# Rope tables and attention bias made in the third projection group, and a gate's blocks spread over three groups, in a one-core transformer layer

## The chip, the core and the metric

The kernel runs on one core of a Trainium2 chip. The core has a matrix engine (TensorE, PE in the profile, its weight loads PEld), a vector engine (VectorE, DVE), a scalar engine (ScalarE, ACT), a general engine (GpSimd, POOL) and a sync engine (SyncE, SP), which here only issues transfers. Each engine runs its own queue in order. The metric is device time in microseconds for one execution. The kernel before took 1390.01 us, the median of three runs (1387.78 to 1391.03).

## The reference

One layer of a diffusion transformer, 256 latent tokens and 256 context tokens of width 2048, all in float32. What matters here:

```python
mod = (silu_c @ w_ada[l] + b_ada[l])[:, None, :]           # 6 segments of 2048: shift, scale, gate, twice
sh_a, sc_a, gt_a, sh_f, sc_f, gt_f = jnp.split(mod, 6, axis=-1)
h  = rms_norm(x,  g_attn[l]) * (1.0 + sc_a)  + sh_a         # latent tokens
hc = rms_norm(xc, g_attn[l]) * (1.0 + csc_a) + csh_a        # context tokens
pl = jnp.split(h @ w_in, offsets, axis=-1)                  # w_in: 2048 x 4928, four head groups
pc = jnp.split(hc @ w_in, offsets, axis=-1)
# neighbourhood attention (bias rpb), grouped queries with rotary, latent attention, differential attention
x = x + gt_a * o_l                                          # gate of the attention: segment 2
h = rms_norm(x, g_ffn[l]) * (1.0 + sc_f) + sh_f             # segments 4 and 3
x = x + gt_f * swiglu(h, ffn_wg[l], ffn_wu[l], ffn_wd[l])   # segment 5
return rms_norm(x, g_final)
```

## The kernel before, in words

Every large product is done in split precision: a weight tile is loaded (512 KB, `raw`), ACT rounds it to a high part (`whi`, L137), DVE subtracts for the low part (`wlo`, L140), and PE makes three passes (L160, L161, L163). Weight tiles go through four `raw` buffers and six `whi`/`wlo` buffers, all loaded from SP's queue.

The input projection of the first head groups (queries, keys and values of the first, queries, keys and values of the second: five blocks of 512 columns, line 437 and `q_block`) is cut along the contraction into five groups, `parts = [[0], [1], [2, 3], [4, 5], [6, 7]]`, each number being a pair of 128-row chunks. Partial sums stay in SBUF and DVE adds each group's to them (L410). While a group runs, the shift and scale of the pairs of the next group are computed on PE (`ada_pe`, L296): a pair needs eight loads of w_ada (L198, "pair loads" below; each is two transfers of 256 KB), the first four into the four buffers `araw`, the next four into the four buffers `o` of another pool, which later hold the rope tables, the bias and the attention outputs. When a pair's shift and scale are there, `modulate` (L309 to L326) makes its normed activations, which the next group's products read.

The segments 2, 4 and 3 of the modulation (the first gate, then scale and shift of the second half) are needed for one token row only and are computed on DVE (`ada_block`): a segment is four blocks of 512 columns, and a block is eight loads of 512 KB ("gate loads" below), each followed by two multiply-adds over 128x512 on DVE (L374; the block's first product is on ACT, L372). `add_ada` puts the blocks in a queue of side tasks. `side.pump` is called after each step of the main work with an estimated cost; a block's next load and its multiply-adds are put into the program each time the estimated clock has moved on by `gap`:

```python
due[0] = max(due[0] + gap, side.now - 4 * gap)
yield 0.0, max(0.0, due[0] - side.now)
```

In the fifth group (`gi == len(parts) - 1`, L530) the kernel before calls `prepare()` (L458) and queues blocks 0 and 1 of the gate with a gap of 2.4, through the `araw` buffers. `prepare` loads the bias, the rope tables, the gains and the mask into `xa` and `xb` (buffers that the tokens have left), and POOL makes from them the tables `tab` and two tiles `bias`, in three of the four `o` buffers. Blocks 2 and 3 and the segments 4 and 3, ten blocks or 80 loads, follow the projection groups with a gap of 2.6 (L670 to L672), through the `raw` buffers that the weights also use. They run beside the attention heads and the remaining projections (`proj`: ML_CQ, DF_Q, ML_CKV, DF_K, DF_V). All of segment 2 must be done at L914, 4 and 3 at L953. The order of instructions on each engine is then settled by a list scheduler, which works with estimated durations.

Of the kernel before, what the change touches and what calls it, by code (L numbers as in the profile page):

```python
# [10 lines left out]
F32 = mybir.dt.float32  # L11
F32R = mybir.dt.float32r
AF = mybir.ActivationFunctionType
ALU = mybir.AluOpType
# [3 lines left out]
P = 128  # L18
# [69 lines left out]
def hybrid_dit_kernel(ctx: ExitStack, tc: tile.TileContext, a, out):  # L88
    nc = tc.nc
    pe, act, dve, pool, sp = nc.tensor, nc.scalar, nc.vector, nc.gpsimd, nc.sync  # L90
# [20 lines left out]
    opool = po.enter_context(tc.tile_pool(name="opool", bufs=1, side="right"))  # L111
# [276 lines left out]
    def add_ada(seg, gap, load, nbs=range(4), ahead=0):  # L388
        due[0] = side.now
        order = [(nb, k2) for nb in nbs for k2 in range(8)]  # L390
        held = {}

        def fetched(nb, k2):

            i = order.index((nb, k2))
            for nb_, k_ in order[i:i + ahead + 1]:
                if (nb_, k_) not in held:
                    c0 = seg * D + nb_ * 512
                    held[nb_, k_] = load(ada_rows[:, 2 * k_:2 * k_ + 2, c0:c0 + 512], [P, 2, 512])
            return held[nb, k2]  # L400

        return [side.add(ada_block(seg, nb, gap, load, fetched), lane="gate", width=1) for nb in nbs]
# [51 lines left out]
    tabs, bias = {}, []  # L454
# [3 lines left out]
    def prepare():  # L458

        xa = sb0.tile([P, 2, 4, S], F32, name="xa", tag="x_t", bufs=2)  # L460
        act.dma_start(xa, a["na_bias"].rearrange("t p h k -> p t h k"))
        xb = sb0.tile([P, D], F32, name="xb", tag="x_t", bufs=2)
        cs128 = xb[:, 0:512].rearrange("p (a t n) -> p a t n", a=2, t=2)
        act.dma_start(cs128[:, 0], a["rope_c128"].rearrange("(t p) n -> p t n", p=P))
        act.dma_start(cs128[:, 1], a["rope_s128"].rearrange("(t p) n -> p t n", p=P))
        gb = xb[:, 512:768].rearrange("p (t n) -> p t n", t=2)
        act.dma_start(gb[:, 0, :], a["gqa_gq"].partition_broadcast(P))
        act.dma_start(gb[:, 1, :], a["gqa_gk"].partition_broadcast(P))
        mask = xb[:, 768:832]
        act.dma_start(mask, a["na_mask"])  # L470
        lv = xb[0:64, 832:836]
        act.dma_start(lv, a["diff_l"].rearrange("t d -> d t"))
        lp = xb[0:64, 836:838]
        dve.tensor_tensor(out=lp, in0=lv[:, 0:2], in1=lv[:, 2:4], op=ALU.mult)
        lps = misc()
        pe.matmul(lps[:, 0:2], lhsT=ones[0:64, 0:1].to_broadcast([64, P]), rhs=lp, start=True, stop=True)
        act.activation(le, lps[:, 0:2], AF.Exp)
        dve.tensor_tensor(out=neglam, in0=le[:, 1:2], in1=le[:, 0:1], op=ALU.subtract)
        dve.tensor_scalar(out=neglam, in0=neglam, scalar1=-0.2, scalar2=None, op0=ALU.add)
        tab = opool.tile([P, 2, 2, 2, 128], F32, name="tab", tag="o", bufs=4)  # L480
        for i, nm in enumerate("qk"):
            cg, sg = tab[:, i, 0], tab[:, i, 1]
            g = gb[:, i:i + 1, :]
            pool.tensor_tensor(out=cg, in0=cs128[:, 0], in1=g.to_broadcast([P, 2, 128]), op=ALU.mult)
            for lo, hi in ((0, 64), (64, 0)):
                pool.tensor_tensor(out=sg[:, :, lo:lo + 64], in0=cs128[:, 1, :, lo:lo + 64], in1=g[:, :, hi:hi + 64].to_broadcast([P, 2, 64]), op=ALU.mult)
            tabs[nm] = (cg, sg)
        for t in range(2):
            b = opool.tile([P, 4, S], F32, name="bias", tag="o", bufs=4)
            bv = b.rearrange("p h (i c) -> p (h i) c", c=64)  # L490
            pool.tensor_tensor(out=bv, in0=xa[:, t].rearrange("p h (i c) -> p (h i) c", c=64), in1=mask.unsqueeze(1).to_broadcast([P, 16, 64]), op=ALU.add)
            bias.append(b)

    def first_group():
# [27 lines left out]
    gate_tasks = []  # L522
    for gi, prs in enumerate(parts):
        nxt = []
        if gi + 1 < len(parts):
            for pr in parts[gi + 1]:
                nxt.append(side.add(ada_pe(pr, wait=(3.0, 1.5, 5.5, 5.5)[gi]), lane="ada", width=1))
                if gi == 0:
                    nxt[-1]["ready"] = side.now + 8.0
        if gi == len(parts) - 1:  # L530
            prepare()
            gate_tasks = add_ada(2, 2.4, ada_raw, (0, 1))
        if gi == 0:
            first_group()
        else:
            q_block(prs, False)
            for c0, units in blocks:
                block(c0, prs, False, units)
        side.finish(*nxt)
        if gi + 1 < len(parts):  # L540
            for pr in parts[gi + 1]:
                modulate(pr)
# [124 lines left out]
        pool.dma_start(g, gd.partition_broadcast(P))  # L667
        return g

    GAP = 2.6  # L670
    gate_tasks = add_ada(2, GAP, stream_raw, (2, 3))
    mod_tasks = add_ada(4, GAP, stream_raw) + add_ada(3, GAP, stream_raw)  # L672

    act.activation(na_qT, na_qT, AF.Copy, scale=128.0 ** -0.5)
    sc_mm = plain_score(na_qT, na_kT, lambda h: h)
# [389 lines left out]
    for gi, (f0, f1) in enumerate(groups):  # L1065
        last = gi == len(groups) - 1
        aT, tasks = {}, {}
        for fb in range(f0, f1):
            ga = gu(a["ffn_wg"], fb) if fb else first_g
            sg = []  # L1070
# [43 lines left out]
    for t in range(2):  # L1114
        for c0, cn in (((0, 512),) if t == 0 else ((0, 256), (256, 256))):
# [5 lines left out]
            c = slice(3 * 512 + c0, 3 * 512 + c0 + cn)  # L1121
# [79 lines left out]
```

## Time and profile before

| | us |
|---|---|
| median of three runs | 1390.01 |
| the profiled execution, its own time | 1391.13 |
| span of its instructions | 1389.3 |
| PE busy | 1344.1 |
| DVE busy | 916.3 |
| ACT busy | 618.9 |
| POOL busy | 60.6 |

The profile is of one execution, and all rows below are of it. PE is busy for 97% of the span, so what can be won is in the few stretches in which it isn't. In the rows of stretches each engine has its busy time and, in brackets, its instructions; then the granted TensorE clock (1.00 is 2.4 GHz), the busy share of the transfer engines and what they moved in GB/s. Times are from the start of the span. The third group runs from 91.16 to 142.84 us, the fourth to 195.50, the fifth to about 247. At 219.67 SP issues the first weight load of ML_CQ and at 369.7 the last of ML_CKV.

### The profile page before, as it was taken

What the parts mean: (1) busy time and instruction counts of PE and PEld (TensorE: products, weight loads), DVE (VectorE), ACT (ScalarE), POOL (GpSimd) and SP (SyncE); (2) the same over time, 40 slices, a digit from 0 to 9 for tenths busy, and PEclk for the clock granted to TensorE, in tenths of its full rate; (3) what the DMA queues carried; (4) which work ended last, traced back from release to release, by engine and by line L of the source; (5) the groups of instructions that cost most, each with busy time, mean ns of one, the idle gap of its engine ahead of it and who ended that gap; (6) DMA issues with size and microseconds to landing.
All of it is one profiled execution on the core that took longest, in us unless ns stands there. A gap on an engine that the chain in (4) does not pass through costs nothing.

```text
span 1389.3 us, 19890 instructions
## 1 busy us (share of the span) xinstructions
PE 1344.1 (97%) x7082; PEld 1088.9 (78%) x7082; DVE 916.3 (66%) x1623; ACT 618.9 (45%) x1180; POOL 60.6 (4%) x78
## 2 busy tenths in 40 slices
PE   6999999988999999999999999999999999999997
PEld 4788878766877587787888888888888888888886
DVE  4474589987787936769697855445555565555575
ACT  4432233553233526548444444444444444444453
POOL 1000030100010000000221000000000000000000
PEclk9999999999999999999999999999999999999999
DMA  9998867577878746445899766666565656666554
GB/s 368 333 360 283 278 225 225 171 253 228 279 229 295 248 134 213 136 126 194 308 371 325 246 188 195 187 194 190 189 196 184 217 180 209 196 186 193 189 171 142
DMA packets 179511, 313.78 MB, mean 226 GB/s; under 512 B 14002, under 2 KB 53972, under 8 KB 178260
## 3 DMA queue, kind: packets, MB, share of 16 engines
q1 hardware_dynamic: 170400, 285.25, 62.7%
q0 software_dynamic: 5664, 24.14, 4.6%
q10 hardware_dynamic: 3348, 3.13, 0.8%
q8 instruction: 55, 0.90, 0.3%
q14 instruction: 44, 0.36, 0.1%
HBM read 310.36 MB, written 2.11 MB: 225 GB/s over the span
## 4 chain that ended last, share of the span: by engine, by line
PE 77%; DVE 10%; DMA 8%; issue 3%; ACT 2%; POOL 1%; ACTq 0%; SPq 0%; POOLq 0%; DVEq 0%
PE acc L160 24%; PE acc L161 23%; PE acc L163 23%; DVE ada_acc L374 3%; DMA raw<-in_w_ada_dram 3%; DVE wlo L140 2%; DMA raw<-in_w_in_dram 2%; PE m L296 2%; POOL rstd L172 1%; PE m L1050 1%; PE m L878 1%; DMA x_t<-in_ctx_dram 1%; PE m L589 1%; ACT whi L137 1%; PE m L640 1%
## 5 line engine op out<-in xcount | busy, mean ns | idle before, releaser
L140 DVE TENSOR_TENSOR wlo<-raw,whi 128x512 fp32r<-128x512 f32 (+1 forms) x764 | 492.5, 683 | 354.2 <-ACT whi L137 348.1
L137 ACT CAST whi<-raw 128x512 fp32r<-128x512 f32 (+1 forms) x764 | 433.7, 615 | 572.6 <-PE acc L161 437.2
L160 PE MATMUL acc<-whi,h_hi 128*128 128x512 f32 x704 | 275.1, 391 | 0.0
L161 PE MATMUL acc<-whi,h_lo 128*128 128x512 f32 x704 | 274.1, 389 | 0.0
L163 PE MATMUL acc<-wlo,h_hi 128*128 128x512 f32 x704 | 190.6, 390 | 0.0
L160 PE MATMUL acc<-whi,h 128*128 128x512 f32 (+1 forms) x416 | 165.4, 402 | 8.0 <-ACT whi L137 5.6
L161 PE MATMUL acc<-whi,h 128*128 128x512 f32 (+1 forms) x416 | 159.1, 385 | 0.0
L163 PEld LDWEIGHTS acc<-wlo,h_hi 128*128 128x128 f32 x704 | 132.2, 188 | 28.0 <-DVE wlo L140 0.5
L161 PEld LDWEIGHTS acc<-whi,h_lo 128*128 128x128 f32 x704 | 132.2, 188 | 27.1
L160 PEld LDWEIGHTS acc<-whi,h_hi 128*128 128x128 f32 x704 | 132.2, 188 | 27.0
L160 PE MATMUL acc<-whi,ah 128*128 128x512 f32 (+1 forms) x364 | 139.0, 383 | 0.0
L161 PE MATMUL acc<-whi,al 128*128 128x512 f32 (+1 forms) x364 | 138.6, 382 | 0.0
L374 DVE SCALAR_TENSOR_TENSOR ada_acc<-raw,cs,ada_acc 128x512 f32<-128x512 f32 x150 | 112.1, 749 | 15.0 <-DMA raw<-in_w_ada_dram 8.3
L163 PE MATMUL acc<-wlo,h 128*128 128x512 f32 (+1 forms) x416 | 117.4, 385 | 1.1 <-DVE wlo L140 1.0
L160 PEld LDWEIGHTS acc<-whi,h 128*128 128x128 f32 x416 | 79.5, 192 | 30.9 <-ACT whi L137 10.5
L163 PE MATMUL acc<-wlo,ah 128*128 128x512 f32 (+1 forms) x364 | 96.2, 382 | 0.0
L161 PEld LDWEIGHTS acc<-whi,h 128*128 128x128 f32 x416 | 80.0, 192 | 13.8 <-issue 1.4
L163 PEld LDWEIGHTS acc<-wlo,h 128*128 128x128 f32 x416 | 76.8, 190 | 17.1 <-DVE wlo L140 3.1
L160 PEld LDWEIGHTS acc<-whi,ah 128*128 128x128 f32 x364 | 68.4, 188 | 13.3
L161 PEld LDWEIGHTS acc<-whi,al 128*128 128x128 f32 x364 | 68.5, 188 | 13.1
L163 PEld LDWEIGHTS acc<-wlo,ah 128*128 128x128 f32 x364 | 67.6, 188 | 13.3
L160 PE MATMUL acc<-whi,o_hi 128*128 128x512 f32 x128 | 51.4, 403 | 0.0
(231 smaller groups left out, 1343.4 us busy)
## 6 DMA issues: line engine op xcount, KB each, us to landing
raw<-in_ffn_wg_dram SPq DMA_DIRECT2D x88, 512.0 KB, 4.4
raw<-in_ffn_wu_dram SPq DMA_DIRECT2D x88, 512.0 KB, 4.2
raw<-in_ffn_wd_dram SPq DMA_DIRECT2D x88, 512.0 KB, 4.2
raw<-in_w_ada_dram SPq DMA_DIRECT2D x80, 512.0 KB, 4.6
raw<-in_w_in_dram SPq DMA_DIRECT2D x72, 512.0 KB, 5.5
araw<-in_w_ada_dram SPq DMA_DIRECT2D x128, 256.0 KB, 5.4
raw<-in_w_out_dram SPq DMA_DIRECT2D x32, 512.0 KB, 3.7
graw<-in_w_ada_dram POOLq DMA_DIRECT2D x32, 512.0 KB, 6.3
```

The costliest lines, as they stand in the source:

```text
L137: act.copy(hi, raw[:, k])
L140: dve.tensor_tensor(out=lo, in0=raw[:, k], in1=hi.bitcast(F32), op=ALU.subtract)
L160: pe.matmul(dst, lhsT=l[0], rhs=r[0], start=start, stop=False)
L161: pe.matmul(dst, lhsT=l[0 if w_left else 1], rhs=r[1 if w_left else 0], start=False, stop=False)
L163: pe.matmul(dst, lhsT=l[1 if w_left else 0], rhs=r[0 if w_left else 1], start=False, stop=stop)
L172: pool.tensor_tensor(out=r[:, :n], in0=v[:, :n], in1=mhalf[:, :n], op=ALU.pow)
L296: pe.matmul(mv[32 * j:32 * j + 32, :P], lhsT=cs32[:, kc, :], rhs=raw[:, kc % 2, j // 2, tsl(j % 2)], start=(kc == 0), stop=(kc == KC - 1), ...
L374: dve.scalar_tensor_tensor(out=acc_, in0=raw[:, kk, :], scalar=cs[:, 0, kc:kc + 1], in1=acc_, op0=ALU.mult, op1=ALU.add)
L589: pe.transpose(ps[:, tsl(j)], src[:, tsl(j)], ident)
L640: pe.matmul(o[:, :S], lhsT=vt(kc)[:, v0:v0 + P], rhs=pT[:, kc, :], start=(kc == 0), stop=(kc == 3))
L878: pe.matmul(sc, lhsT=df_qT[hb, h, tsl(t)], rhs=df_kT[h // 2][hb, h % 2, :], start=True, stop=True)
L1050: pe.transpose(ps[:, tsl(j)], src[:, tsl(j)], ident)
```

## The change

`prepare` is called in the third group instead of the fifth. It now makes the tables and the bias where their inputs lie, in `xb` and `xa`, on POOL as before. A new function `keep`, called in the fifth group, copies them into the three `o` buffers on ACT. Blocks 0 and 1 of the gate are queued in the third group with a gap of 7.0, block 2 in the fifth with a gap of 3.0 (all through `araw`), and block 3 and the segments 4 and 3 after the groups with gaps of 3.6, 3.6 and 2.8 (were 2.6).

```diff
-        tab = opool.tile([P, 2, 2, 2, 128], F32, name="tab", tag="o", bufs=4)
+        tab = xb[:, 1024:2048].rearrange("p (i s t n) -> p i s t n", i=2, s=2, t=2)
...
+        for t in range(2):
+            bv = xa[:, t].rearrange("p h (i c) -> p (h i) c", c=64)
+            pool.tensor_tensor(out=bv, in0=bv, in1=mask.unsqueeze(1).to_broadcast([P, 16, 64]), op=ALU.add)
+        return xa, xb
+
+    def keep(xa, xb):
+
+        tab = opool.tile([P, 2, 2, 2, 128], F32, name="tab", tag="o", bufs=4)
+        act.copy(tab.rearrange("p i s t n -> p (i s t n)"), xb[:, 1024:2048])
+        for i, nm in enumerate("qk"):
+            tabs[nm] = (tab[:, i, 0], tab[:, i, 1])
         for t in range(2):
             b = opool.tile([P, 4, S], F32, name="bias", tag="o", bufs=4)
-            bv = b.rearrange("p h (i c) -> p (h i) c", c=64)
-            pool.tensor_tensor(out=bv, in0=xa[:, t].rearrange("p h (i c) -> p (h i) c", c=64), in1=mask.unsqueeze(1).to_broadcast([P, 16, 64]), op=ALU.add)
+            act.copy(b, xa[:, t])
             bias.append(b)
...
+        if gi == 2:
+            made = prepare()
+            gate_tasks = add_ada(2, 7.0, ada_raw, (0, 1))
         if gi == len(parts) - 1:
-            prepare()
-            gate_tasks = add_ada(2, 2.4, ada_raw, (0, 1))
+            keep(*made)
+            gate_tasks += add_ada(2, 3.0, ada_raw, (2,))
...
-    GAP = 2.6
-    gate_tasks = add_ada(2, GAP, stream_raw, (2, 3))
-    mod_tasks = add_ada(4, GAP, stream_raw) + add_ada(3, GAP, stream_raw)
+    gate_tasks = add_ada(2, 3.6, stream_raw, (3,))
+    mod_tasks = add_ada(4, 3.6, stream_raw) + add_ada(3, 2.8, stream_raw)
```

On SP's queue in the third and fourth group, first as it was and then as it is (L125 loads weights, L198 are pair loads, two rows of `x2` each half a pair, L276 are gate loads):

```order
L125 DMA raw<-in_w_in_dram 128x2x512 x4
L198 DMA araw<-in_w_ada_dram 128x2x256 x8
L125 DMA raw<-in_w_in_dram 128x2x512
L198 DMA araw<-in_w_ada_dram 128x2x256 x8
L125 DMA raw<-in_w_in_dram 128x2x512 x4
```

```order
L125 DMA raw<-in_w_in_dram 128x2x512 x4
L276 DMA araw<-in_w_ada_dram 128x2x512 x4
L198 DMA araw<-in_w_ada_dram 128x2x256 x4
L125 DMA raw<-in_w_in_dram 128x2x512
L198 DMA araw<-in_w_ada_dram 128x2x256 x4
L125 DMA raw<-in_w_in_dram 128x2x512
L198 DMA araw<-in_w_ada_dram 128x2x256 x8
L125 DMA raw<-in_w_in_dram 128x2x512 x4
```

Four gate loads come ahead of a pair's first half; there are four such rounds, two in the third group and two in the fourth, and the pair loads behind them wait for the `araw` buffers that the gate loads' multiply-adds on DVE release.

On DVE's queue at the end of the third group, first as it was and then as it is (`gq_k`, `gq_v` and `kT` are partial sums, L309 begins the modulation for the next group):

```order
L410 TENSOR_TENSOR gq_k<-acc,gq_k 128x256
L410 TENSOR_TENSOR gq_v<-acc,gq_v 128x256
L140 TENSOR_TENSOR wlo<-raw,whi 128x512 x3
L410 TENSOR_TENSOR kT<-acc,kT 128x512 x3
L140 TENSOR_TENSOR wlo<-raw,whi 128x512
L410 TENSOR_TENSOR kT<-acc,kT 128x512
L309 TENSOR_TENSOR scg<-m,colA_147 128x4
```

```order
L374 SCALAR_TENSOR_TENSOR ada_acc<-araw,cs,ada_acc 128x512
L410 TENSOR_TENSOR gq_k<-acc,gq_k 128x256
L374 SCALAR_TENSOR_TENSOR ada_acc<-araw,cs,ada_acc 128x512
L410 TENSOR_TENSOR gq_v<-acc,gq_v 128x256
L374 SCALAR_TENSOR_TENSOR ada_acc<-araw,cs,ada_acc 128x512
L140 TENSOR_TENSOR wlo<-raw,whi 128x512
L374 SCALAR_TENSOR_TENSOR ada_acc<-araw,cs,ada_acc 128x512 x2
L140 TENSOR_TENSOR wlo<-raw,whi 128x512
L374 SCALAR_TENSOR_TENSOR ada_acc<-araw,cs,ada_acc 128x512
L140 TENSOR_TENSOR wlo<-raw,whi 128x512
L374 SCALAR_TENSOR_TENSOR ada_acc<-araw,cs,ada_acc 128x512 x2
L410 TENSOR_TENSOR kT<-acc,kT 128x512 x3
```

Eight multiply-adds now stand between the last partial sums of one block and the first of the next.

On SP's queue in DF_Q, first as it was and then as it is (`w_in` rows are weight loads, `w_ada` rows are gate loads):

```order
L125 DMA raw<-in_w_in_dram 128x2x512
L125 DMA raw<-in_w_ada_dram 128x2x512 x2
L125 DMA raw<-in_w_in_dram 128x2x512
L125 DMA raw<-in_w_ada_dram 128x2x512 x2
L125 DMA raw<-in_w_in_dram 128x2x512
L125 DMA raw<-in_w_ada_dram 128x2x512 x3
L125 DMA raw<-in_w_in_dram 128x2x512
```

```order
L125 DMA raw<-in_w_in_dram 128x2x512
L125 DMA raw<-in_w_ada_dram 128x2x512
L125 DMA raw<-in_w_in_dram 128x2x512
L125 DMA raw<-in_w_ada_dram 128x2x512
L125 DMA raw<-in_w_in_dram 128x2x512
L125 DMA raw<-in_w_ada_dram 128x2x512 x2
L125 DMA raw<-in_w_in_dram 128x2x512
```

Fewer gate loads stand between two weight loads. From the first weight load of ML_CQ to the last of ML_CKV there were 44 of them and are 30; in DF_K there were 33 and are 28; in DF_V there were 5 and are 14.

## Rows read from the trace of the kernel before

**Rows 1.** The page: the chain that ended last, by engine.

```profile
PE 77%; DVE 10%; DMA 8%; issue 3%; ACT 2%; POOL 1%; ACTq 0%; SPq 0%; POOLq 0%; DVEq 0%
```

**Rows 2.** Busy time by stretch: stretch, length, engines, clock, transfers.

```profile
75.00:100.00 25.00, 24.86 (x242) 21.02 (x242) 21.93 (x48) 10.31 (x19) 0.00 (x0) 1.00 1.03 374
91.16:142.84 51.68, 51.54 (x467) 42.70 (x465) 27.76 (x53) 13.43 (x25) 0.00 (x0) 1.00 0.87 293
142.84:195.50 52.66, 52.66 (x476) 43.69 (x475) 35.52 (x65) 14.88 (x28) 6.49 (x7) 1.00 0.81 271
195.50:219.67 24.17, 21.14 (x104) 17.36 (x103) 23.46 (x39) 10.33 (x18) 4.85 (x2) 0.86 0.62 196
219.67:369.68 150.01, 137.44 (x645) 106.80 (x644) 133.01 (x269) 64.03 (x137) 9.37 (x8) 0.98 0.69 224
369.68:470.00 100.32, 94.80 (x463) 75.03 (x463) 81.52 (x155) 37.90 (x86) 3.60 (x4) 0.97 0.81 263
470.00:525.00 55.00, 55.00 (x244) 41.38 (x243) 27.00 (x47) 20.62 (x45) 0.00 (x0) 1.00 0.54 172
```

**Rows 3.** The chain between 219.67 and 369.68 us, by line.

```profile
by line: DVE ada_acc L374 17.8%; DMA raw<-in_w_ada_dram 15.0%; DMA raw<-in_w_in_dram 13.5%; DVE wlo L140 9.2%; issue 8.4%; POOL rstd L172 3.9%; PE acc L160 2.8%; PE m L731 2.5%; DVE st L616 2.5%; PE acc L161 2.4%; PE acc L163 2.1%; DVE m L6
```

**Rows 4.** What ACT waited for from 219.67 to 369.68: us, times, longest.

```profile
ACT whi L137 <- DMA raw<-in_w_in_dram: 28.1, 14, 3.8
```

**Rows 5.** What SP waited for from 219.67 to 369.68.

```profile
SPq L125 <- DVE wlo L140: 66.0, 26, 8.8
```

**Rows 6.** Transfers issued from 219.67 to 369.68: count, size, median us to landing.

```profile
raw<-in_w_ada_dram SPq DMA_DIRECT2D x40, 512.0 KB, 4.5
raw<-in_w_in_dram SPq DMA_DIRECT2D x16, 512.0 KB, 4.7
raw<-in_w_in_dram SPq DMA_DIRECT2D x7, 320.0 KB, 3.9
araw<-in_w_ada_dram SPq DMA_DIRECT2D x2, 512.0 KB, 5.6
```

**Rows 7.** PE's wait from 195.5 to 219.67.

```profile
PE acc L160 <- DVE kT L410: 3.0, 2, 1.6
```

**Rows 8.** DVE in order of time, 194 to 204.

```profile
195.87 2.26 DVE L374 SCALAR_TENSOR_TENSOR ada_acc<-araw,cs,ada_acc 128x512 f32<-128x512 f32 x1
198.06 0.68 DVE L410 TENSOR_TENSOR kT<-acc,kT 128x512 f32<-128x512 f32 x1
198.66 2.24 DVE L374 SCALAR_TENSOR_TENSOR ada_acc<-araw,cs,ada_acc 128x512 f32<-128x512 f32 x1
```

**Rows 9.** The multiply-adds of L374 alone, from 219.67 to 369.68.

```profile
219.67:369.68 150.01, 61.96 (x83) 0.98 0.69 224
```

**Rows 10.** POOL in order of time, 194 to 201: start, us, instruction.

```profile
194.76 5.59 POOL L491 TENSOR_TENSOR bias<-xa,xb 128x1024 f32<-128x1024 f32 x2
```

**Rows 11.** Transfers from 91.16 to 142.84: bytes and mean rate.

```profile
DMA packets 12668, 15.16 MB, mean 293 GB/s; under 512 B 746, under 2 KB 9847, under 8 KB 12663
```

**Rows 12.** The first gate loads on SP, 177 to 187.

```profile
180.05 6.78 SPq L276 DMA_DIRECT2D araw<-in_w_ada_dram  x5
```

**Rows 13.** ACT in order of time, 184 to 197.

```profile
184.93 0.72 ACT L372 ACTIVATE ada_acc<-araw,cs 128x512 f32<-128x512 f32 x1 [1.74 <-DMA araw<-in_w_ada_dram]
...
190.28 0.27 ACT L299 COPY mvs<-m 128x128 f32<-128x128 f32 x1 [1.64 <-PE m L296]
195.00 1.14 ACT L137 CAST whi<-raw 128x512 fp32r<-128x512 f32 x2 [4.46 <-PE acc L161]
```

**Rows 14.** ACT's issue of the mask, 58 to 63.6.

```profile
60.87 0.33 ACTq L470 DMA_DIRECT2D xb<-in_na_mask_dram  x1
```

**Rows 15.** DVE in order of time, 68 to 78.

```profile
74.12 1.38 DVE L140 TENSOR_TENSOR wlo<-raw,whi 128x512 fp32r<-128x512 f32 x2 [2.73 <-ACT whi L137]
```

**Rows 16.** An ACT pass over 128x1024.

```profile
212.28 1.06 ACT L674 ACTIVATE qT<-qT 128x1024 f32<-128x1024 f32 x1
```

**Rows 17.** PE's use of that `mvs` tile.

```profile
195.49 0.14 PEld L302 LDWEIGHTS m<-ident,mvs 128*128 128x128 f32 x1
```

More of the change, by code (lines that the diff above doesn't have):

```diff
@@ L486, in prepare @@
                 pool.tensor_tensor(out=sg[:, :, lo:lo + 64], in0=cs128[:, 1, :, lo:lo + 64], in1=g[:, :, hi:hi + 64].to_broadcast([P, 2, 64]), op=ALU.mult)
-            tabs[nm] = (cg, sg)
+        for t in range(2):
[7 more added lines that the diff above has]
+            tabs[nm] = (tab[:, i, 0], tab[:, i, 1])
         for t in range(2):
             b = opool.tile([P, 4, S], F32, name="bias", tag="o", bufs=4)
-            bv = b.rearrange("p h (i c) -> p (h i) c", c=64)
-            pool.tensor_tensor(out=bv, in0=xa[:, t].rearrange("p h (i c) -> p (h i) c", c=64), in1=mask.unsqueeze(1).to_broadcast([P, 16, 64]), op=ALU.add)
+            act.copy(b, xa[:, t])
             bias.append(b)
```

## The prediction

> **What bounds the kernel now.** I read the chain that ended last first. Three quarters of it are PE, then come DVE and the transfers [rows 1], and POOL has 1%. PE is busy for 1344.1 of 1389.3 us, so all that this change can win without touching a matmul is in 45.2 us, and the next view must say where they are. That is the table by stretch [rows 2]. The third and fourth group have almost none: PE idles 51.68 - 51.54 = 0.14 us and 0.00 us. The opening of the fifth has 24.17 - 21.14 = 3.03 us. The stretch of the attention heads and the first remaining projections, 219.67 to 369.68, has 150.01 - 137.44 = 12.57 us. The next hundred microseconds have 5.52, and 470 to 525 has none.
>
> In the long stretch I then read the chain by line: the multiply-adds of the gate loads 17.8%, the gate loads themselves 15.0%, the weight loads 13.5% [rows 3]. So loads in flight and their consumers end last there, not PE. The waits say the same from two sides: ACT waited 28.1 us for weights to land [rows 4], and SP waited 66.0 us for a raw buffer that DVE's subtraction had not released [rows 5]. The transfer engines are busy for 69% only; it is the ring of four buffers that is tight. In the transfers 40 + 2 gate loads stand beside 16 + 7 weight loads [rows 6], so 65 loads in 150.01 us, 2.31 us each.
>
> **The opening of the fifth group.** PE waited 3.0 us, twice, for an addition to kT [rows 7]. Two multiply-adds just ahead of these additions took 2.26 and 2.24 us [rows 8] in place of 61.96/83 = 0.75 us [rows 9], while POOL made its two bias passes, 5.59 us from 194.76 on [rows 10]. That is 1.51 + 1.49 = 3.0 us, the whole of PE's wait. POOL's passes leave this place, and ten multiply-adds of block 1 stand ahead of the modulation on DVE where twelve stood. I take -2.5 us; the bounds are 0 (these multiply-adds hold kT back just as long by their number) and -4 (3.03 and something of the following clock, which is 0.86 in this stretch).
>
> **The long stretch.** Its gate loads fall from 42 to some 30 (SP's order has 44 and 30 between the two weight loads that mark its ends; the trace's stretch holds 42 of the 44). If every load went on taking 2.31 us, 30 + 23 = 53 loads would take 122.3 us, 27.7 less; but PE's own work is 137.44 us, so the stretch can't shrink by more than 12.57 us unless PE's work gets shorter too, as it would if its clock (0.98) or its pipelining gained. DVE loses 12 x 2 x 0.7465 = 17.9 us, from 133.01 to 115.1, and 115.1/137.4 is 84%, which no longer binds. On the other side the chain also holds pieces that aren't side work: DVE's softmax steps, POOL's rstd, issue [rows 3]. If these filled the place of the loads, nothing would be won. I take most of PE's idle time and a little of the faster matmul stream, -12 us, between 0 and -27.7. The value is near the 12.57, since that is the row that PE itself gives.
>
> **Behind it.** In 369.68 to 470 there are five loads fewer (33, now 28) of 5.52 us of idle time; I take -0.5 us. From 470 to 525 nine more stand (5, now 14): 9 x 2 x 0.7465 = 13.4 us on DVE, which is busy for 27.0 of 55.0 us. PE's 55.0 busy us hide it: 0. If that cover were gone, the price would be those 13.4 us.
>
> **The third and fourth group.** Here the cost must lie. A gate load is 0.524 MB, so eight add 4.19 MB to the third group's 15.16 MB [rows 11]: 19.35 MB. The rate that this kernel held over 75 to 100 us is 374 GB/s [rows 2]; by it they need 51.7 us, exactly what the group takes. By 293 GB/s at a share of 0.87 the engines would be full at 337 GB/s and need 57.4 us, +5.7 us. The fourth group moved 0.271 x 52.66 = 14.3 MB, and with eight gate loads where some five stood, 1.6 MB more, it fits by either.
>
> The rate of 374 GB/s was held for 25 us [rows 2]. The Trainium skill's page "DMA: Bandwidth & Descriptors", section Specifications, puts the memory limit of one core at about 358 GB/s. By it 19.35 MB would need an estimated 54.05 us, 2.4 us more than the group takes; by the row it costs nothing. This trace goes above the page's figure, so the row stands.
>
> What the change adds is a wait. The pair loads on SP now stand behind four gate loads and want the same `araw` buffers, which DVE's multiply-adds release. Behind the waiting pair load are four weight loads, and PE needs those. On DVE the first multiply-add of a round waits for ACT's first product (L372) and that for the transfer; behind it stand evacuations (gq_k, gq_v, kT), wlo and the modulation. On ACT whi stands behind L372. Today five gate loads issued from 180.05 on [rows 12] gave ACT its input 4.88 us later, at 184.93, after an idle 1.74 us [rows 13]. A round is thus 4.9 us of landing and 8 x 0.7465 = 6.0 us on DVE, some 11 us; four rounds fit in 104 us, and DVE goes from 27.76 to some 39 busy us out of 51.68. I take +2 us in all for late weights or late partial sums, from 0 to +5.7.
>
> **POOL's passes, at another place.** The last of their inputs, the mask, was issued at 60.87 [rows 14]; with a gate load's 4.9 us it is there by 66, and `xa` and `xb` are free. So they should run between some 65 and 77 us, where DVE makes wlo (at 74.12, already 2.73 us after whi [rows 15]). One bias pass, 5.59/2 = 2.8 us, is the most that one wlo can be held by. I take +0.5 us, from 0 to +2.8.
>
> **The copies on ACT.** The copies are three of 128x1024, 1.06 us each by the nearest pass of that size [rows 16], 3.2 us. Two of them stand ahead of the copy of mvs, which ended at 190.28 + 0.27 [rows 13] and is used at 195.49 [rows 17]. With 2.1 us ahead it ends at 192.7, still in time, and ACT idled 4.46 us before its next rounding at 195.00 [rows 13]. So 0, at most +1.
>
> **The sum.** -2.5 - 12 - 0.5 + 0 + 2 + 0.5 + 0 = -12.5 us. The profiled execution's own time is 1391.13 us, 1.1 above the median of 1390.01. Its sum gives 1378.6, brought to the median 1377.5. I predict 1378 us.
>
> **The rivals.** *The relief is lost.* The long stretch is held by its own chains: statistics, softmax steps and the ring of buffers, in which one slow wlo holds the next load (8.8 us at worst [rows 5]). For it speaks that the rows of loads make up only 46% of the chain; against it, that DVE's share is 89% now. Then only the opening's 2.5 us are won and the groups' 2.5 us spent: 1390 to 1391 us.
>
> *More than the idle time.* If the time per load stays near 2.31 us and the waits of PE shrink in the matmul stream as well, the stretch gives 20 us, halfway to its bound and beyond PE's idle row: -2.5 - 20 - 0.5 + 2.5 = -20.5, 1370 us, 1369 from the median. For it speaks that SP waited 66.0 us for buffers; against it that the clock is already 0.98.
>
> *The rounds stall PE.* One mechanism: SP waits in order on a pair load until DVE has released `araw`, DVE waits until the gate loads have landed, and the four weight loads behind come late. It decides at PE's loss per round: four rounds that cost more than (15 + 2.8)/4 = 4.4 us each eat the gains of 2.5 + 12 + 0.5 and 0.2% of the time more. At 5 us each it is 1391.1 - 15 + 20 = 1396 us. For it speaks the third group's share of 0.87 in the transfer engines; against it that a round needs 11 of 26 us, and that PE idled 0.14 us in a group whose SP was already in order behind the same buffers.
>
> **Chances.** The forecast has 0.60, the lost relief 0.13 (of it 0.10 within 0.2%, which is about what a measurement of this kernel can tell from no change, and 0.03 faster), more than the idle time 0.17, the stalling rounds 0.10. So faster 0.80, same 0.10, slower 0.10. The range is 1366 to 1391 us, the forecast's own 1372 to 1386. The low end is -4 in the opening and -20 in the stretch; the high end takes in the lost relief, and also a stretch that gives 4 us with +5.7 in the groups (1390.0 - 2.5 - 4 - 0.5 + 5.7 = 1388.7). Left out are the stalls, 0.10, and some 0.07 of still larger gains.
>
> **What would show it.** In the new profile PE's idle time from the fifth group's first product to ML_CQ's first weight load should be below 1 us with no multiply-add above 1 us there; the long stretch should have about 53 loads and PE's idle time at 1 to 3 us, with DVE near 84%; the third and fourth group should lose at most 2 us in PE; POOL's passes should stand near 65 to 77 us and the copies between 188 and 195 us. Idle time of PE in the third or fourth group, ended by whi or by a partial sum, of more than 4 us per round makes the forecast wrong; so does a long stretch that is as long as before with fewer loads.

## The result and the profile after

The changed kernel takes 1371.42 us, the median of four runs (1368.11 to 1373.65), against 1389.65 us of the kernel before on the same chip. The ratio is 0.9868 (95% interval 0.9848 to 0.9887), so it is 18 us faster; 1378 us were predicted, in a range of 1366 to 1391. The profiled execution took 1373.65 us, 17.5 less than the profiled one of before.

To see where the time went I cut both executions where PE had been given the same matmuls. Each matmul counts with the usual pitch of its form, and the table gives the time that each kernel took for the same piece of PE's work. It is worked out from the start times of all PE instructions in the traces. In the kernel before the cuts fall at 187.9, 236.2, 399.0, 514.8 and 664.6 us, in the kernel after at 188.0, 229.9, 375.6, 497.0 and 647.3:

```
piece (us of PE's own work)            before     after
start to the end of the 4th group       179.4     179.6    +0.2
opening of the fifth group               48.3      41.9    -6.4
fifth group, heads, up to DF_Q          162.8     145.7   -17.1
the rest of the projections             115.8     121.4    +5.6
output projection                       149.8     150.3    +0.5
all the rest                            715.0     714.8    -0.2
```

The rows of the same view as [rows 2], of the kernel after: stretch, length, busy times of PE, PEld, DVE, ACT and POOL, clock, transfers. The last row is the long stretch by the same two weight loads, which SP now issues at 212.68 and 340.67.

```profile
91.16:142.84 51.68, 51.40 (x466) 42.48 (x466) 37.93 (x69) 15.31 (x29) 0.00 (x0) 1.00 0.92 315
142.84:195.50 52.66, 52.66 (x478) 43.80 (x477) 40.64 (x77) 18.59 (x31) 0.00 (x0) 1.00 1.00 351
195.50:219.67 24.17, 24.17 (x133) 20.97 (x132) 24.00 (x44) 9.98 (x17) 0.00 (x0) 1.00 0.77 252
212.68:340.67 127.99, 123.86 (x594) 99.04 (x593) 115.44 (x240) 63.54 (x137) 10.29 (x8) 1.00 0.66 212
```

The third group idles 0.28 us of PE and the fourth none, although DVE has some 10 and 5 us more work there and the transfer engines are busy for all of the fourth. In the opening PE idles no more, and its clock is 1.00 where it was 0.86. In the long stretch PE's idle time is 4.1 us where it was 12.57, and the clock is 1.00.

The opening, in DVE's order of time (start, us, instruction), which answers to [rows 8]:

```profile
191.66 1.54 DVE L374 SCALAR_TENSOR_TENSOR ada_acc<-araw,cs,ada_acc 128x512 f32<-128x512 f32 x2
193.11 0.69 DVE L410 TENSOR_TENSOR kT<-acc,kT 128x512 f32<-128x512 f32 x1
193.90 0.75 DVE L374 SCALAR_TENSOR_TENSOR ada_acc<-araw,cs,ada_acc 128x512 f32<-128x512 f32 x1
194.56 0.69 DVE L410 TENSOR_TENSOR kT<-acc,kT 128x512 f32<-128x512 f32 x1
```

A multiply-add there takes 0.75 us again. POOL has done its passes long before; they stood here, from 194.76 on [rows 10]. ACT's copies stand where the order put them, with that of `mvs` after two of them [rows 13]. POOL's view, then ACT's:

```profile
66.72 4.72 POOL L489 TENSOR_TENSOR xa<-xa,xb 128x1024 f32<-128x1024 f32 x2
```

```profile
190.13 1.05 ACT L495 COPY tab<-xb 128x1024 f32<-128x1024 f32 x1 [0.71 <-PE m L296]
191.08 1.05 ACT L500 COPY bias<-xa 128x1024 f32<-128x1024 f32 x1
192.03 0.26 ACT L299 COPY mvs<-m 128x128 f32<-128x128 f32 x1
192.18 1.06 ACT L500 COPY bias<-xa 128x1024 f32<-128x1024 f32 x1
```

In the long stretch, 212.68 to 340.67, the transfers issued [rows 6], and after them what ACT [rows 4] and SP [rows 5] waited for (us, times, longest):

```profile
raw<-in_w_ada_dram SPq DMA_DIRECT2D x29, 512.0 KB, 4.2
raw<-in_w_in_dram SPq DMA_DIRECT2D x16, 512.0 KB, 4.6
raw<-in_w_in_dram SPq DMA_DIRECT2D x7, 320.0 KB, 3.7
```

```profile
ACT whi L137 <- DMA raw<-in_w_in_dram: 14.6, 11, 2.8
```

```profile
SPq L125 <- DVE wlo L140: 47.6, 22, 7.6
```

The same 23 weight loads stand beside 29 gate loads where there were 42, and the waits for them fall from 28.1 to 14.6 us and from 66.0 to 47.6.

### The profile page after: what moved, and what is told of

It is laid out like the page before. It is cut to its first block, busy times and chain, and to the rows that moved or that the text cites. A ratio compares the mean times of both kernels' runs of the same rounds, so it can differ in the third digit from the quotient of the medians.

```text
span 1371.9 us, 19891 instructions
## 1 busy us (share of the span) xinstructions
PE 1333.6 (97%) x7082; PEld 1085.9 (79%) x7082; DVE 914.3 (67%) x1623; ACT 621.6 (45%) x1183; POOL 56.4 (4%) x78
## 4 chain that ended last, share of the span: by engine, by line
PE 63%; DMA 3%; DVE 3%; ACT 1%; issue 1%; POOL 0%; POOLq 0%; DVEq 0%; ACTq 0%
PE acc L160 20%; PE acc L161 20%; PE acc L163 20%; DMA raw<-in_w_ada_dram 2%; DVE ada_acc L374 1%; DVE wlo L140 1%; PE m L1061 1%; DMA raw<-in_w_in_dram 1%; DMA raw<-in_ffn_wg_dram 1%; PE m L905 1%; PE m L889 1%; PE m L601 0%; ACT whi L137 0%; DMA raw<-in_w_out_dram 0%; PE m L652 0%
## 5 line engine op out<-in xcount | busy, mean ns | idle before, releaser
L160 PE MATMUL acc<-whi,h 128*128 128x512 f32 (+1 forms) x416 | 161.8, 392 | 1.2 <-DVE ropet L620 0.7
L161 PE MATMUL acc<-whi,h 128*128 128x512 f32 (+1 forms) x416 | 158.1, 382 | 0.0
L374 DVE SCALAR_TENSOR_TENSOR ada_acc<-raw,cs,ada_acc 128x512 f32<-128x512 f32 x135 | 101.1, 749 | 37.6 <-DMA raw<-in_w_ada_dram 25.5
```

What stands on the lines that cost most here:

```text
L160: pe.matmul(dst, lhsT=l[0], rhs=r[0], start=start, stop=False)
L161: pe.matmul(dst, lhsT=l[0 if w_left else 1], rhs=r[1 if w_left else 0], start=False, stop=False)
L374: dve.scalar_tensor_tensor(out=acc_, in0=raw[:, kk, :], scalar=cs[:, 0, kc:kc + 1], in1=acc_, op0=ALU.mult, op1=ALU.add)
```

## The experiments

For all kernels the same table of pieces was worked out (us; the last column is the median with the ratio to the kernel before on the same chip and its interval):

```
                      4th group  opening  heads  rest of proj.  out proj.  median, ratio (95%)
before                  179.4     48.3    162.8     115.8        149.8
after                   179.6     41.9    145.7     121.4        150.3     1371.4  0.9868 (0.9848-0.9887)
tables_alone            180.2     42.9    159.9     116.9        149.8     1381.7  0.9960 (0.9947-0.9973)
gate_alone              179.6     45.9    144.0     118.9        149.2     1375.0  0.9916 (0.9900-0.9931)
gaps_alone              179.3     49.3    146.7     123.0        158.8     1391.9  1.0037 (1.0025-1.0049)
old_gaps                180.3     41.9    159.4     119.3        149.4     1385.0  0.9973 (0.9959-0.9986)
half_multiplies         180.2     49.0    144.7     115.8        149.6     1374.8  0.9905 (0.9893-0.9918)
half_loads              180.5     49.0    146.3     113.4        149.8     1373.7  0.9895 (0.9879-0.9911)
fifth_buffer            178.5     48.4    152.2     115.9        150.6     1378.8  0.9936 (0.9914-0.9958)
third_block_early       183.0     44.2    148.6     118.2        150.0     1379.7  0.9940 (0.9928-0.9952)
wider_gaps              179.6     41.9    144.1     116.1        159.5     1380.5  0.9938 (0.9922-0.9955)
wide_then_tight         179.4     42.6    147.4     116.1        149.8     1368.9  0.9869 (0.9847-0.9890)
after_fifth_buffer      179.7     41.9    140.6     115.2        149.8     1364.7  0.9828 (0.9809-0.9847)
both                    178.8     42.3    146.8     115.6        150.5     1367.5  0.9864 (0.9844-0.9885)
```

The pieces are of one profiled execution each, which can stand some us from its kernel's median: from 2.9 us above it (*tables_alone*, 1384.57) to 4.4 below (*wider_gaps*, 1376.16). The verdicts rest on the medians, the pieces tell where the time went. How far a piece can go by chance shows in two rows of the table: *wider_gaps* and *wide_then_tight* have the same instructions in the same order on SP, DVE, ACT and PE up to 423 us, and their heads took 144.1 and 147.4 us. A difference of some 3 us in one piece of one execution therefore shows nothing by itself.

### The two parts apart

*tables_alone* is the changed kernel with the gate as before:

```diff
-            gate_tasks = add_ada(2, 7.0, ada_raw, (0, 1))
...
-            gate_tasks += add_ada(2, 3.0, ada_raw, (2,))
+            gate_tasks = add_ada(2, 2.4, ada_raw, (0, 1))
...
-    gate_tasks = add_ada(2, 3.6, stream_raw, (3,))
-    mod_tasks = add_ada(4, 3.6, stream_raw) + add_ada(3, 2.8, stream_raw)
+    gate_tasks = add_ada(2, 2.6, stream_raw, (2, 3))
+    mod_tasks = add_ada(4, 2.6, stream_raw) + add_ada(3, 2.6, stream_raw)
```

> The tables and the bias made in place in the third group and copied by ScalarE, as in the changed kernel; the gate's blocks 0 and 1 in the fifth group and a gap of 2.6 behind it, as before. Theory: POOL's passes beside DVE held the additions to kT, PE idled 3 us and then ran at a granted clock of 0.81 for some 16 us, so this part alone gives the 6.2 us that the opening of the fifth group lost: 1383 to 1384 us, clock 1.00 from 200 to 216 us. Rival: the multiply-adds of the gate standing ahead of kT hold it by their number, which stays: 1388 us or more, and the clock falls again.

*gate_alone* is the kernel before with the blocks and gaps of the changed one:

```diff
+        if gi == 2:
+            gate_tasks = add_ada(2, 7.0, ada_raw, (0, 1))
...
-            gate_tasks = add_ada(2, 2.4, ada_raw, (0, 1))
+            gate_tasks += add_ada(2, 3.0, ada_raw, (2,))
...
-    gate_tasks = add_ada(2, GAP, stream_raw, (2, 3))
-    mod_tasks = add_ada(4, GAP, stream_raw) + add_ada(3, GAP, stream_raw)
+    gate_tasks = add_ada(2, 3.6, stream_raw, (3,))
+    mod_tasks = add_ada(4, 3.6, stream_raw) + add_ada(3, 2.8, stream_raw)
```

> The gate's blocks and gaps as in the changed kernel, prepare() in the fifth group as before. Theory that the two parts add up: the long stretch gives its 16 us, behind it some 5 are lost again, the opening stays at a loss of some 6: 1378 us. Rival: taking 16 gate loads out of the fifth group does all of it, since POOL then disturbs nobody: 1371 to 1373 us.

The tables alone gave 5.4 us of the opening's 6.4, and 6.4 in all by the medians, where 6.2 were expected. The median lies 1.3 us beyond the theory's end, since the kernel before took 1388.0 us on this chip; the rival's 1388 or more is out. The gate alone gave 18.8 us in the heads and 2.4 in the opening, lost 3.1 behind the heads, and stands at 1375.0 us, between the two expectations. The parts nearly add up: 6 and 13 us against 18.

What had the opening cost? In the kernel before PE waited twice for kT. The first matmul after each wait, with the wait in brackets (start, us, instruction):

```profile
198.79 0.39 PE L160 MATMUL acc<-h,whi 128*128 128x256 f32 x1 [1.59 <-DVE kT L410]
201.65 0.76 PE L160 MATMUL acc<-whi,h 128*128 128x512 f32 x1 [1.44 <-DVE kT L410]
```

Its stretches up to 199.10 us and from there to 205.92, then two stretches of *tables_alone*:

```profile
195.50:199.10 3.60, 2.01 (x13) 1.50 (x12) 3.60 (x4) 2.10 (x4) 3.60 (x2) 1.00 0.81 265
199.10:205.92 6.82, 5.38 (x15) 3.79 (x14) 6.82 (x15) 1.13 (x2) 1.25 (x1) 0.50 0.26 85
```

```profile
195.50:204.00 8.50, 8.12 (x48) 6.56 (x47) 8.50 (x20) 3.95 (x7) 0.00 (x0) 1.00 0.70 240
204.00:213.00 9.00, 9.00 (x52) 7.88 (x52) 8.93 (x16) 4.18 (x7) 0.00 (x0) 1.00 0.81 266
```

In the kernel before PE first waits 1.59 us for kT, and 0.3 us after that wait its granted clock falls to 0.50, the lower of its two levels, until 205.92; the second wait lies inside. The 5.38 us of matmuls there would have been 2.7 at full clock, so up to 2.7 us went to the clock, on top of the 3.0 that PE waited. Without the passes of POOL beside DVE, PE idles 0.38 us there and the clock is 1.00. In *gate_alone*, where POOL's passes stay beside DVE, a multiply-add took up to 2.69 us, where 0.75 is usual, and PE waited again, 2.6 us in three pieces of at most 0.98, for kT and for wlo. Here the clock stayed 1.00:

```profile
195.26 2.69 DVE L374 SCALAR_TENSOR_TENSOR ada_acc<-araw,cs,ada_acc 128x512 f32<-128x512 f32 x1
```

### Number or pace of the gate loads

*gaps_alone* is the kernel before with the new gaps, *old_gaps* the changed kernel with the old ones:

```diff
-    gate_tasks = add_ada(2, GAP, stream_raw, (2, 3))
-    mod_tasks = add_ada(4, GAP, stream_raw) + add_ada(3, GAP, stream_raw)
+    gate_tasks = add_ada(2, 3.6, stream_raw, (2, 3))
+    mod_tasks = add_ada(4, 3.6, stream_raw) + add_ada(3, 2.8, stream_raw)
```

> The kernel before with the gaps 3.6, 3.6 and 2.8 in the place of 2.6 and nothing else; all 80 gate loads stay behind the groups. If the pace of the gate loads beside the weight loads sets the long stretch: it gets shorter by 10 us or more there, and what of it is left at the end depends on whether the loads that are pushed back hurt: 1378 to 1384 us. If their number does: 1389 to 1393 us, no gain.

```diff
-    gate_tasks = add_ada(2, 3.6, stream_raw, (3,))
-    mod_tasks = add_ada(4, 3.6, stream_raw) + add_ada(3, 2.8, stream_raw)
+    gate_tasks = add_ada(2, 2.6, stream_raw, (3,))
+    mod_tasks = add_ada(4, 2.6, stream_raw) + add_ada(3, 2.6, stream_raw)
```

> The changed kernel with a gap of 2.6 behind the groups as before; 72 gate loads there in place of 80. If the pace sets the stretch, most of its 16 us are lost and only the opening's 6 are left: 1382 to 1385 us. If the number does: 1371 to 1374 us, and the 5 us lost behind 400 us come back.

The gaps alone take 16.1 us off the heads with all 80 loads still behind the groups. 72 loads at the old gap take 3.4 off, but *tables_alone* took 2.9 off with all 80 at that gap, so nothing is shown for the number; by the medians, on the same chip, *old_gaps* is the slower of the two (1385.0 and 1381.7 us). So the pace sets the stretch, not the number. But the gaps alone gave back 7.2 us in the rest of the projections and 9.0 in the output projection, and the whole is 0.37% slower than before: within what was expected if the number counts, but for another reason. The transfers that *gaps_alone* issues from the first load of w_out on, 502.7 to 560 us, show why:

```profile
raw<-in_w_out_dram SPq DMA_DIRECT2D x13, 512.0 KB, 4.4
raw<-in_w_ada_dram SPq DMA_DIRECT2D x10, 512.0 KB, 4.2
```

Ten gate loads now lie in the output projection; in the kernel before none does, and none in the changed one. Summed, the gaps were 80 x 2.6 = 208 us before, are 48 x 3.6 + 32 x 2.8 = 262 us here and 40 x 3.6 + 32 x 2.8 = 234 us in the changed kernel. Taking block 2 from behind the groups, for which blocks 0 and 1 made room in the fifth, is therefore what pays for the wider gaps.

### DVE, transfers or buffers

What does a gate load hold, if its pace matters? I left out half of its arithmetic, then half of its transfers, and then gave the ring a buffer, each time in the kernel before.

```diff
-            for kk in range(2):
+            for kk in range(1 if load is stream_raw else 2):
```

> The kernel before, with all its gate loads, but behind the groups each load is followed by one multiply-add in place of two: half of the gate's products are left out there. If DVE holds the raw buffers and through them the weight loads: the long stretch loses 10 us or more of its idle time, 1374 to 1379 us. If the loads themselves (their transfer and their place in the ring of four) do: 3 us or less, 1385 to 1388 us.

```diff
-            raw = fetched(nb, k2) if fetched else load(ada_rows[:, 2 * k2:2 * k2 + 2, c0:c0 + 512], [P, 2, 512])
+            if k2 % 2 == 0 or load is not stream_raw:
+                raw = fetched(nb, k2) if fetched else load(ada_rows[:, 2 * k2:2 * k2 + 2, c0:c0 + 512], [P, 2, 512])
```

> The kernel before, with all its multiply-adds, but behind the groups only every second gate load is made and its tile is used twice: half of the gate's weights are left out there. If the loads set the stretch: 10 us or more are won, 1374 to 1379 us. If DVE does: 3 us or less, 1385 to 1388 us.

```diff
-        raw = stream.tile(shape, F32, name="raw", tag="raw", bufs=4)
+        raw = stream.tile(shape, F32, name="raw", tag="raw", bufs=5)
...
-        gr = small.tile([16, P], F32, name="gr", bufs=1)
+        gr = stream.tile([P, 512], F32, name="ada_acc", bufs=2)[0:16, 0:P]
...
-        raw = stream.tile([P, nk_, 4, hi - lo], F32, name="raw", tag="raw", bufs=4)
+        raw = stream.tile([P, nk_, 4, hi - lo], F32, name="raw", tag="raw", bufs=5)
```

> The kernel before with five raw buffers in place of four (a small tile moves into another pool to make room); loads, multiply-adds and gaps are those of before. If a gate load holds PE up by the buffer it keeps from its issue to its last multiply-add, one more buffer gives 8 us or more in the long stretch, and the opening keeps its loss: 1375 to 1381 us. If DVE's throughput or the transfers' does, a buffer gives 3 us or less: 1386 to 1389 us.

Both halves won what both theories claimed for themselves alone, 18.1 and 16.5 us in the heads. The middle of that piece, where the kernel before lost most, tells how that can be. Nearly the same part of PE's work (219 to 230 matmuls), in the kernel before, then in *half_multiplies*, *half_loads*, *fifth_buffer*, and in the kernel after:

```profile
286.10:348.70 62.60, 52.57 (x219) 38.05 (x220) 50.33 (x91) 30.00 (x66) 1.99 (x3) 0.95 0.74 240
```

```profile
284.90:337.20 52.30, 49.77 (x230) 37.83 (x230) 35.08 (x69) 30.74 (x69) 1.10 (x2) 1.00 0.86 297
```

```profile
286.30:338.10 51.80, 49.62 (x225) 36.59 (x224) 49.11 (x91) 29.83 (x65) 2.79 (x3) 1.00 0.61 192
```

```profile
285.40:339.70 54.30, 49.93 (x225) 36.64 (x224) 48.81 (x90) 29.46 (x65) 2.38 (x3) 1.00 0.83 274
```

```profile
278.10:328.60 50.50, 47.61 (x221) 36.68 (x220) 42.99 (x80) 31.36 (x70) 1.48 (x2) 1.00 0.76 250
```

With half of the loads DVE does all of its work and is busy for 49.11 of 51.80 us, 95%, and PE idles 2.2 us: DVE's throughput was not the bound at 80%. With half of the multiply-adds the transfers run at 0.86 and 297 GB/s, and PE idles 2.5: nor were they at 0.74 and 240. With five buffers nothing is left out, both are busier, and 8.3 us of the 62.6 go. So neither throughput binds. What is left is the ring of buffers: a gate load holds a buffer from its issue over its landing to its last multiply-add, and the load behind it in SP's order waits for that. SP's waits in that piece of the kernel before (us, times, longest) show a buffer held by a gate load's multiply-adds and one held by a weight tile's subtraction, in like amounts:

```profile
SPq L125 <- DVE ada_acc L374: 21.6, 17, 1.9
SPq L125 <- DVE wlo L140: 20.2, 10, 6.2
```

By this reading either half shortens or thins the hold, and so does a wider gap. In the heads the fifth buffer gives 10.6 us where the halves and the gaps give 16 to 18, so it shows the greater part of it; what the rest hangs on the runs don't separate.

PE's side of it, in the same piece of the kernel before (us, times, longest):

```profile
PEld acc L160 <- ACT whi L137: 8.4, 9, 3.1
...
PE acc L160 <- ACT whi L137: 5.1, 6, 2.7
```

and with the fifth buffer:

```profile
PEld acc L160 <- ACT whi L137: 4.7, 7, 1.8
...
PE acc L160 <- ACT whi L137: 2.1, 2, 1.4
```

In the kernel after no such row is left in that piece. The fifth buffer moves one small tile as well; that this tile did anything was not tested apart.

### Where more could be had

*third_block_early* takes a third block into the groups:

```diff
-            gate_tasks = add_ada(2, 7.0, ada_raw, (0, 1))
+            gate_tasks = add_ada(2, 5.0, ada_raw, (0, 1, 2))
...
-            gate_tasks += add_ada(2, 3.0, ada_raw, (2,))
+            gate_tasks += add_ada(2, 3.0, ada_raw, (3,))
...
-    gate_tasks = add_ada(2, 3.6, stream_raw, (3,))
-    mod_tasks = add_ada(4, 3.6, stream_raw) + add_ada(3, 2.8, stream_raw)
+    mod_tasks = add_ada(4, 4.0, stream_raw) + add_ada(3, 3.4, stream_raw)
```

> The changed kernel with block 2 in the third group as well (blocks 0 to 2, gap 5.0), block 3 in the fifth (gap 3.0), and 64 gate loads behind the groups at gaps of 4.0 and 3.4. If fewer gate loads per weight load is all that counts and the groups still hide the rounds: another 2 to 5 us in the stretch and behind it, 1366 to 1370 us. If the transfers of the fourth group, busy for 1.00 of it already, have no room: PE idles there by 5 us or more, 1375 us or more.

Against the changed kernel it costs 3.4 us in the groups, 2.3 in the opening and 2.9 in the heads, and it has 3.2 less behind them; by the medians it is 8 us slower, with fewer loads and wider gaps behind the groups. The groups' piece stands out, since every other kernel has 178.5 to 180.5 there, and PE idles 1.5 us more from 91.2 to 195.5 us. In the groups the weights come late: ACT waited 23.9 us for them from 119 to 192 us, against 9.1 in the changed kernel.

```profile
ACT whi L137 <- DMA raw<-in_w_in_dram: 23.9, 4, 9.6
```

Whether the transfers had no room or SP's order put the weights late is not told apart: the transfer engines were busy for 1.02 from 119 to 142.84 us, but for 0.92 from 169.4 to 195.5, where they were at 1.02 in the changed kernel.

*wider_gaps* (4.2, 4.2, 2.8), *wide_then_tight* (4.2, 4.2, 2.2), *after_fifth_buffer* (the changed kernel with the edit of *fifth_buffer*) and *both* (that with 4.2, 4.2, 2.2) differ from the changed kernel in the numbers alone or in the buffer:

> The changed kernel with gaps of 4.2 in place of 3.6 behind the groups, the last segment's 2.8 kept. If the pace still holds PE in the stretch: 1 to 3 us won there. If the loads that this pushes behind it come late for the norm before the second half, as they did with the gaps alone: 4 us or more are lost between 490 and 560 us, 1374 us or more.

> The changed kernel with gaps of 4.2 for block 3 and the first of the two segments, and 2.2 in place of 2.8 for the last. The wider gaps gave 3 to 7 us of the stretch up to 470 us and lost 10 behind it by lateness. With the last 32 loads closer the sum of the gaps is 238 us, near the 234 of the changed kernel: if lateness was all that cost, 1366 to 1370 us. If the closer loads hold the weight loads again between 380 and 500 us: 1373 us or more.

> The changed kernel with five raw buffers in the same way. Where the change has already taken the loads' share out of the long stretch, PE's idle time there no longer hangs on a buffer: 1369 to 1373 us. If buffers still hold weight loads: 3 us or more are won, 1366 to 1368 us.

> The changed kernel with five raw buffers and the gaps 4.2, 4.2 and 2.2 together. Each alone took 7 and 2 to 3 us off the changed kernel. If they win the same idle time, a weight load that waits for a buffer: 1363 to 1366 us, no more than the buffer alone. If they add up: 1361 to 1362 us.

The wider gaps show no gain in the heads (1.6 us, within chance), take 5.3 us less behind them, and lose 9.2 in the output projection, into which eight gate loads slip. The transfers from its first load of w_out on, 484.7 to 560 us:

```profile
raw<-in_w_out_dram SPq DMA_DIRECT2D x17, 512.0 KB, 5.0
raw<-in_w_ada_dram SPq DMA_DIRECT2D x8, 512.0 KB, 4.9
```

With the last segment tighter only two slip, and that loss is gone: 1368.9 us, but its ratio is that of the changed kernel, so no gain is shown. The fifth buffer in the changed kernel gives another 5.1 us in the heads and 6.2 behind them: 1364.7 us, ratio 0.9828 (0.9809 to 0.9847), the fastest of all; its interval just clears the changed kernel's, which was measured on another chip, and its profiled execution, from which the pieces are, ran 2.8 us below its median. I had expected the ring to be relieved by then; it still held weight loads. With both edits it is 1367.5 us: the two do not add. The heads took 146.8 us there, against 140.6 with the buffer alone, but the intervals of the two ratios just overlap. Why is open; the runs don't say.

## Why the prediction was right, and where its steps were not

The time was 6.6 us below the forecast and in the range, but the steps were right to different degrees. The opening and the long stretch gave 3.9 and 5.1 us more than their terms and the part behind took 6.1 back, so that the sum came as near as it did is in part luck.

*The opening* was to give 2.5 us, at most 4; it gave 6.4. The mechanism was right: passes of POOL beside DVE stretch the multiply-adds ahead of kT. The term was mis-sized, because I took the value below the 3.03 us that PE idled and put the clock down to a part of 1 us, though 0.86 stood in the row [rows 2]: 24.17 us at 0.86 instead of 1.00 are 3.4 us. Where a low clock stands beside a wait, it is part of what can be won, and its row has it.

*The long stretch* was to give 12 us, and the piece of PE's work that holds it gave 17.1; it ends at 399.0, where my stretch ended at 369.68. The piece before and after:

```profile
236.20:399.00 162.80, 146.01 (x701) 114.51 (x700) 139.14 (x292) 71.20 (x164) 12.97 (x12) 0.96 0.69 223
```

```profile
229.90:375.60 145.70, 138.02 (x699) 112.92 (x698) 120.82 (x261) 70.60 (x163) 12.41 (x12) 0.99 0.67 212
```

PE's idle time fell from 16.79 to 7.68 us, 9.1 of the 17.1, and its busy time from 146.01 to 138.02, the other 8.0. The clock has some 5 of these by an estimate from the two rows (0.04 x 162.8 less 0.01 x 145.7). So the idle time gave less than the 12.57 us that I had put in nearly whole, and the matmul stream, which I gave "a little", nearly as much as the idle time. Part of it may be chance: the mean granted clock of the profiled execution of before is 0.989, and the other executions of that kernel have 0.989 to 0.995.

The step's reason was wrong besides. I counted loads and DVE's share (89%, then 84%): the share was no bound, as 95% in *half_loads* shows. In the changed kernel it didn't fall at all, it is 90% of the long stretch (115.44 of 127.99 us), and PE's idle time went down all the same. Fewer loads at the old pace give 3.4 us (*old_gaps*, hardly more than chance) where the pace by itself gives 16.1 (*gaps_alone*). What the change altered was the pace, by its gaps, and what it relieved were, for the greater part, the buffers. I had read SP's 66.0 us of waiting for buffers [rows 5] and the ring of four, and then priced the change by DVE's busy time. Of the rivals, "more than the idle time" named the right row but not the pace; its 1369 us is within 3 us of the result.

*Behind it* I had -0.5 and 0 us; it cost 5.6 us. PE idles 6.4 of 121.40 us there in the kernel after, 1.3 of 115.80 before. It isn't the number of gate loads, 35 there and 33 before. PE waits in short pieces for softmax steps of ACT and DVE, and for a block's end:

```profile
375.60:497.00 121.40, 114.98 (x528) 86.58 (x527) 87.81 (x153) 45.19 (x94) 0.00 (x0) 1.00 0.72 231
```

```profile
PEld m L601 <- ACT p L642: 2.3, 3, 0.9
...
PEld m L601 <- ACT p L630: 1.9, 1, 1.9
PEld m L601 <- DVE mcol L382: 1.6, 1, 1.6
...
PE m L601 <- DVE st L631: 1.5, 1, 1.5
```

What puts these steps late is not settled: the same gate in *gate_alone* cost 3.1 us there, *old_gaps* 3.5, while *wider_gaps* cost 0.3, and a part of the 5.6 can be chance. The buffers have a share here too: the fifth buffer in the changed kernel brings the piece to 115.2 us and PE's idle time to 1.5.

```profile
370.50:485.70 115.20, 113.71 (x528) 86.75 (x527) 87.73 (x153) 45.44 (x94) 0.00 (x0) 1.00 0.75 247
```

And I had not asked what happens at the end of the queue at all. In the kernel after SP issues the last of these gate loads at 488.6 us and the first load of w_out at 490.2, so the deadline was within reach, as *gaps_alone* and *wider_gaps* show, 9 us each.

*The groups* were to cost 2 us and cost 0.2. My 19.35 MB in the third group did not come about:

```profile
DMA packets 12174, 16.26 MB, mean 315 GB/s; under 512 B 716, under 2 KB 7817, under 8 KB 12169
```

The gate loads pushed pair loads into the fourth group, which now moves 0.351 x 52.66 = 18.5 MB where it moved 14.3. The two took 5.3 MB more between them without loss, and the fourth at a share of 1.00. The limit of some 358 GB/s that the Trainium skill's page "DMA: Bandwidth & Descriptors" states (Specifications) was not tested by the change: 351 were held over 52.66 us, just below it. By the 374 over 25 us [rows 2] it doesn't hold here. More loads than this cost time in *third_block_early*, whether for want of room or by SP's order. The rival of stalling rounds falls with the same rows: the two rounds that each group took cost PE 0.28 us in the third and none in the fourth. (Between the last gq_v and the first kT of the third group stand six multiply-adds; the eight that I named are those of the whole excerpt.)

*POOL's passes* ran from 63.6 to 71.4 us, a little before the 65 to 77 forecast, and cost nothing that can be told from the groups' 0.2 us. They did hold one instruction of DVE, though none that PE needed; in the kernel after, then in the one before:

```profile
66.89 2.22 DVE L474 TENSOR_TENSOR xb<-xb 64x2 f32<-64x2 f32 x1 [2.25 <-DMA xb<-in_diff_l_dram]
```

```profile
68.85 0.15 DVE L474 TENSOR_TENSOR xb<-xb 64x2 f32<-64x2 f32 x1 [3.90 <-DMA xb<-in_diff_l_dram]
```

I had misread [rows 15]: its 2.73 us are what DVE idled until whi came, not a delay of wlo behind whi. *The copies* ran from 190.1 to 193.2, in the opening, where PE idled no more.

## What to carry to other kernels

Where loads of two kinds share a ring of buffers on one in-order queue, price a change by how long each load holds its buffer and by how far apart the loads of the second kind stand, not by the busy share of the engine that consumes them. A slower pace needs a longer run-up: ask first when the last of the slowed loads is due, and move some of them ahead of the queue to pay for it. Beside a wait in front of the matmuls read the clock of the rows that follow: here 3.0 us of waiting came with 3.4 us of slower matmuls, and in *gate_alone* 2.6 us came with a clock of 1.00.

## What the runs showed of the hardware

Three multiply-adds of 128x512 on DVE took 2.24, 2.26 and 2.69 us while POOL made passes over SBUF of 128x1024, where 0.75 us is usual. That is no factor: a 64x2 instruction took 2.22 us beside such a pass and 0.15 without, and the additions to kT, 128x512, took 0.68 us with or without. POOL's own two passes took 5.59 us beside the multiply-adds and 4.72 us at 66.72 us, where DVE had little to do. In one kernel a wait of PE of 1.59 us ended at 198.79 us, and from 199.10 to 205.92 the granted clock was 0.50, the lower of its two levels, with a second wait of 1.44 us inside; in *gate_alone* three waits of 0.78 to 0.98 us at the same place left it at 1.00. The transfer engines held 351 GB/s over 52.66 us without a wait that PE would have seen.
